# A hybrid decoder block: two more weight chunks by seven block products, and a longer split tail of the mixing layer

## The chip, the core and the metric

The kernel runs on one core of one Trainium2 chip. The metric is device time in microseconds (us) of one execution, as the median over runs. Five engines run their own instruction streams: PE (matmuls, with its weight loads shown apart as PEld), DVE, ACT and POOL for element-wise work, SP for issuing DMAs. They wait for one another by semaphores.

## The reference

One block of a decoder, 256 tokens, width 2048, all in float32. Cut to what matters here:

```python
h = rms_norm(x, norm_mix_pre)
z = h @ w_in                                     # 2048 x 11280: pool, q, k, v, low-rank gate, r, branch gates
y_a = pool_mixer(p) @ w_branch_a
o = rms_norm(gla_chunked(q, k, v, log_a), gla_norm) * silu(r)
y_b = o @ w_branch_b                             # 2048 x 2048
gates = sigmoid(gate_logits + b_branch_gates)
mixed = (gates[0] * y_a + gates[1] * y_b) @ w_out   # 2048 x 2048
x = x + rms_norm(mixed, norm_mix_post)
h = rms_norm(x, norm_ffn_pre)
f = (silu(h @ w_ffn_gate) * (h @ w_ffn_up)) @ w_ffn_down   # width 5632 between
x = x + rms_norm(f, norm_ffn_post)
```

Nearly all of the work is matrix products of the 256 tokens with large weights that are read once from memory.

## The kernel before

**Precision.** An operand is kept as two parts, a rounded high part and the remainder (`wh` and `wl` of a weight, a pair ending in h and l of an activation such as `m3h`, `m3l`). A product is three matmuls: high by high, high by the weight's remainder, and the activation's remainder by the weight's high part (lines 381 to 383 and 441 to 443). So every weight tile must be copied to `wh` by ACT (L343 or L417) and subtracted to `wl` by DVE (L347 or L421) before PE can use it.

**Jobs.** `plan()` cuts each weight into chunks of 512 columns. A chunk is a job; the order of the jobs is the order of the lists there (gates, w_branch_b, w_out, then the FFN). The weight has 16 tiles of 128 rows in k. A plain job (`fast` false) has eight steps of two k tiles each; a step multiplies both halves of the tokens (t0 and t1, 128 each) with matmuls of 512 columns: 2 k tiles x 2 halves x 3 = 12 matmuls.

**Seven block products.** A job with `fast` true takes its first eight k tiles otherwise. Tokens, k and columns are each split in two, and instead of the eight block products of that 2x2x2 cut, seven products of sums of blocks are formed, named q1, q2, q4, q6, q7, r3, r5 (class `Part`). Each is 4 k tiles x 3 = 12 matmuls of 256 columns. The sums on the weights' side are one accumulating DMA (L413, POOL's queue) and three DVE additions (L402, L404, L406); those on the activations' side are formed once per activation (`combine`). The other eight k tiles stay four steps, now with matmuls of 256 columns, 24 per step. Weights of the parts arrive as two tiles per job (`blocks`, three buffers, L1058), those of a step as one tile (`raw`, three buffers, L334); each load is 0.5 MB (512 KB), eight of them per job in either form, 4 MB in all. q1, r5, q6 and q7 are the EARLY parts: they are put between the last units of the job before (`merged`), the rest into the job's own list (`units`).

**Order and buffers.** The loop at the end of the kernel walks the units in order, and before each it prepares weights up to four units ahead, since `wh` and `wl` have four buffers (`BUFS`): the conversion of a unit waits until PE has ended the unit four before it. `blocks()` loads the next job's blocks up to twelve units ahead, when one of the three buffers is free. `done` work (evictions) is issued when a half of the tokens has its last unit; `after` and `bg` spread transposes and other side work over later units. A list scheduler of the framework then places the instructions of each engine; each engine executes its list in that order.

**The end of w_out.** `out_done` squares a chunk's result (ACT, L889) and scales it by a broadcast row (DVE, L890). In the last chunk (n = 3, here out3) `tail=3` makes the last three steps run for t0 first, all three, and then for t1. When t0 is complete, `first_residual` and `residual_part` turn t0's rows into the residual `xr` (power on POOL L211, then L913), transpose them on PE (L204, `tr<-ident,xr`) and split them into `h20h`, `h20l` and so on (L243, L244), which the first FFN gate chunk multiplies. That chunk has `head=4`: its first four steps run for t0, then for t1. In the following, out0 to out3 are the chunks of w_out, b0 to b3 those of w_branch_b, w0 to w3 the last four steps of out3, s0 to s3 the first four steps of the first FFN gate chunk.

Of the kernel before, what the change touches and what calls it, by code (L numbers as in the profile page):

```python
# [26 lines left out]
CW = 512  # L27
# [35 lines left out]
def plan():  # L63

    kt = D // P
    for kind, off, order in [("p", OFF_P, (0, 1)), ("r", OFF_R, (1, 2, 3, 0)), ("q", OFF_Q, (0, 1)), ("k", OFF_K, (0, 1))]:
        for i in order:
            low = kind == "r" and i == 0
            yield (kind, i, "w_in", 0, kt, OFF_G if low else off + i * CW, CW + RANK if low else CW,
                   kind == "r" and i > 1)  # L70
    for n in range(4):
        yield "a", n, "w_branch_a", 0, kt // 2, n * CW, CW, False
    for n in range(4):
        yield "v", n, "w_in", 0, kt, OFF_V + n * CW, CW, n > 0
    for n in range(8):
        yield "gates", n, "w_in", 0, kt, OFF_GA + n * CW, CW, n != 3
    for n in range(4):
        yield "b", n, "w_branch_b", 0, kt, n * CW, CW, n in (1, 3)
    for n in range(4):
        yield "out", n, "w_out", 0, kt, n * CW, CW, n < 3  # L80
    chunks = DFF // CW
    for part in range(3):
        ms = range(part * 4, min(part * 4 + 4, chunks))
        for m in ms:
            yield "gate", m, "w_ffn_gate", 0, kt, m * CW, CW, m > 0
            yield "up", m, "w_ffn_up", 0, kt, m * CW, CW, m > 0
        for n in range(4):
            yield "down", (part, n), "w_ffn_down", part * 16, 4 * len(ms), n * CW, CW, (part, n) != (2, 3)


def packed(name, w):

    import numpy as np

    out = []
    for _, _, which, k0, kt, c0, width, fast in plan():
        if which != name:
            continue
        rows = w[0, k0 * P:(k0 + kt) * P, c0:c0 + width].reshape(kt, P, width)
        if fast:  # L100
            for b in range(2):
                blocks = rows[b * 4:b * 4 + 4].reshape(4, P, 2, HW)
                out.append(blocks.transpose(2, 1, 0, 3).ravel())
            rows = rows[4 * FAST:]
        out.append(rows.reshape(-1, GK, P, width).transpose(0, 2, 1, 3).ravel())
    return np.concatenate(out)
# [3 lines left out]
def tile_hybrid_block(ctx: ExitStack, tc: tile.TileContext, *aps):  # L110
# [35 lines left out]
    def scratch():  # L146
        return scr.tile([P, CW], F32, tag="scr", name=nm("scr"))
# [81 lines left out]
    class Act:  # L229


        def __init__(self, name, groups, tag):
            self.name = name
            self.hi = [placed(his, (4, T), f"{tag}{g}h", f"{name}{g}h") for g in range(groups)]
            self.lo = [placed(los, (4, T), f"{tag}{g}l", f"{name}{g}l") for g in range(groups)]
# [48 lines left out]
    class Job:  # L284
# [5 lines left out]
        def __init__(self, w, at, kt, width, fast, lhs, done, across=False, head=0, tail=0, begin=None):  # L290
            self.w, self.at, self.lhs, self.kt, self.width, self.done = w, at, lhs, kt, width, done
            self.across, self.groups, self.ps, self.extra, self.fast = across, kt // GK, None, None, fast
            self.begin = begin
            both = tuple(range(NT))
            self.blocks = []
            self.early = [Part(self, n) for n in EARLY] if fast else []
            w = [Step(self, g) for g in range(FAST * 4 // GK if fast else 0, self.groups)]
            m = [(w[g], (t,)) for t in both for g in range(head)]
            m += [(x, both) for x in w[head:len(w) - tail]]
            m += [(x, (t,)) for t in both for x in w[len(w) - tail:]]  # L300
            self.units = m
            if fast:
                q2, q4, r3 = [(Part(self, n), both) for n in ("q2", "q4", "r3")]
                self.units = [q2, m[0], q4, r3] + m[1:] if len(m) > 2 else [q2, q4, r3] + m
            for w, ts in self.units:
                w.uses += 1

        def merged(self, early):

            e = [(p, (0, 1)) for p in early]  # L310
            u = self.units
            if not e:
                if self.fast and u[1][0].part:
                    u = [u[0], u[3], u[1], u[2]] + u[4:]
                return u
            if self.fast and u[1][0].part:
                return [u[0], e[0], u[1], e[1], u[2], e[2], u[3], e[3]] + u[4:]
            if self.fast:
                return u[:3] + [e[0], u[3], e[1], u[4], e[2], u[5], e[3]] + u[6:]
            u, v = u[:-4], u[-4:]  # L320
            return u + [x for pair in zip(e, v) for x in pair]
# [182 lines left out]
    def all_but_last(part, tag):  # L504
        s = one.tile([P, NT], F32, tag="ss", name=nm("ss"), bufs=2)
        dve.tensor_reduce(s, part[:, :, :3], axis=mybir.AxisListType.X, op=ALU.add)
        rs[tag] = one.tile([P, NT], F32, tag=f"ms{tag}", name=f"ms{tag}")
        dve.tensor_scalar(rs[tag], s, EPS, None, op0=ALU.add)
# [295 lines left out]
    mix = {}  # L804
# [15 lines left out]
    def broadcast(v):  # L820
        b = st.tile([P, CW], F32, tag="bc", name=nm("bc"), bufs=1)
        pool.dma_start(b, v[None, :].to_broadcast([P, CW]))
        return b
# [22 lines left out]
    def yb_done(n):  # L846
        def done(j, ts):
            if not mix:
                mix["m"] = Act("m", 4, "A")
            nat = []  # L850
            for t in ts:
                y, g = chunk(ya, t, n, "Y", "ya"), chunk(gb, t, n, "X", "gb")
                dve.tensor_tensor(g, g, j.ps[t], op=ALU.mult)
                dve.tensor_tensor(y, y, g, op=ALU.add)
                nat.append(y)
            if n == FAST - 1:
                after(3, lambda: bg.extendleft(reversed(mix["m"].combine())))
            for i in (0, 1):
                after(1 + i, lambda i=i: to_operand(mix["m"], n, nat, (i,)))
        return done  # L860
# [18 lines left out]
    def out_done(n):  # L879
        def done(j, ts):  # L880
            c = slice(n * CW, (n + 1) * CW)
            if n not in bcs:
                bcs[n] = broadcast(norm_mix_post[0, c])
            for t in ts:
                if mg[t] is None:
                    mg[t] = rest.tile([P, D], F32, tag=f"Y{t}", name=f"mg{t}")
                    xr[t] = one.tile([P, D], F32, tag=f"X{t}", name=f"xr{t}")
                    sync.dma_start(xr[t], x[0, t * P:(t + 1) * P, :])
                act.activation(scratch(), j.ps[t], AF.Square, scale=D ** -0.5, accum_out=part1[:, t, n:n + 1])  # L889
                dve.tensor_tensor(mg[t][:, c], j.ps[t], bcs[n], op=ALU.mult)  # L890
                if n == 3:
                    first_residual(t)
            if n == 2:
                all_but_last(part1, "1")
        return done

    def first_residual(t):
        r = one.tile([P, 1], F32, tag=f"rstd1{t}", name=f"rstd1{t}")
        power(r, part1[:, t, 3:], rs["1"][:, t:t + 1])
        if not h2:  # L900
            h2["h"] = Act("h2", 4, "B")
        for c in range(4):
            bg.append(lambda c=c: residual_part(t, c, r))
        if t == NT - 1:
            for c in range(4):
                bg.append(lambda c=c: squares(xr, part2, (0, 1), (c,), f32(h2["h"].lo[3][:, 3, T - 1:])))
            bg.append(second_rstd)
            bg.append(lambda: bg.extendleft(reversed(h2["h"].combine())))
# [28 lines left out]
    def ffn_gate_done(m):  # L937
        def done(j, ts):
            for t in ts:
                s = scratch()  # L940
                act.activation(s, j.ps[t], AF.Silu, scale=rz(t, "f"))
                sil[m, t] = s
        return done
# [54 lines left out]
    def finish(t, last, ps):  # L998
# [15 lines left out]
        "v": lambda n: dict(lhs=lambda: hT, done=v_done(n)),  # L1014
        "gates": lambda n: dict(lhs=lambda: hT, done=gate_done(*divmod(n, 4))),
        "b": lambda n: dict(lhs=lambda: oT["o"], done=yb_done(n)),
        "out": lambda n: dict(lhs=lambda: mix["m"], done=out_done(n), tail=3 * (n == 3)),
        "gate": lambda m: dict(lhs=lambda: h2["h"], done=ffn_gate_done(m), head=4 * (m == 0)),
        "up": lambda m: dict(lhs=lambda: h2["h"], done=ffn_up_done(m)),
        "down": lambda pn: dict(lhs=lambda: fa[pn[0]], done=down_done(*pn), tail=4 * (pn == (2, 3)),  # L1020
# [4 lines left out]
    for kind, n, name, k0, kt, c0, width, fast in plan():  # L1025
        jobs.append(Job(source[name], at[name], kt, width, fast, **kinds[kind](n)))
        at[name] += kt * P * width
# [132 lines left out]
```

## Time and profile before

| | us |
|---|---|
| three runs | 1464.76, 1464.86, 1468.63 |
| median | 1464.86 |
| the profiled execution | 1465.09 |
| its span, first to last instruction | 1463.3 |
| PE busy in it | 1439.8 |
| DVE busy in it | 1237.3 |
| ACT busy in it | 912.6 |

The profiled execution is one run of its own; 1.8 us of its time lie outside of its span. The granted clock of PE in it is 0.999 of full speed. Busy time of PE is that of overlapping instructions, so that starts of successive matmuls, and not their lengths, tell its pace.

### The profile page before, as it was taken

What the parts mean: (1) busy time and instruction counts of PE and PEld (TensorE: products, weight loads), DVE (VectorE), ACT (ScalarE), POOL (GpSimd) and SP (SyncE); (2) the same over time, 40 slices, a digit from 0 to 9 for tenths busy, and PEclk for the clock granted to TensorE, in tenths of its full rate; (3) what the DMA queues carried; (4) which work ended last, traced back from release to release, by engine and by line L of the source; (5) the groups of instructions that cost most, each with busy time, mean ns of one, the idle gap of its engine ahead of it and who ended that gap; (6) DMA issues with size and microseconds to landing.
All of it is one profiled execution on the core that took longest, in us unless ns stands there. A gap on an engine that the chain in (4) does not pass through costs nothing.

```text
span 1463.3 us, 28065 instructions
## 1 busy us (share of the span) xinstructions
PE 1439.8 (98%) x11404; PEld 1380.5 (94%) x11404; DVE 1237.3 (85%) x1390; ACT 912.6 (62%) x1192; POOL 71.3 (5%) x96
## 2 busy tenths in 40 slices
PE   8999999999999999999999999999999999999997
PEld 8999999889999899989978999999999999999996
DVE  6785568898999987899778899888989899889996
ACT  6465744556675665466557666666666666666664
POOL 2000000000100000000000000000000000000000
PEclk9999999999999999999999999999999999999999
DMA  8746566736678588648854777777766777777654
GB/s 292 261 138 218 170 218 204 240 101 215 205 221 255 187 258 265 199 168 284 265 173 159 225 221 222 225 230 235 242 215 212 224 227 232 232 238 227 205 182 149
DMA packets 89489, 316.02 MB, mean 216 GB/s; under 512 B 10204, under 2 KB 10928, under 8 KB 89104
## 3 DMA queue, kind: packets, MB, share of 16 engines
q1 hardware_dynamic: 77616, 278.89, 55.3%
q0 software_dynamic: 8448, 29.64, 10.8%
q10 hardware_dynamic: 3296, 5.71, 1.1%
q8 instruction: 89, 1.46, 0.4%
q14 instruction: 40, 0.33, 0.1%
HBM read 284.84 MB, written 4.19 MB: 198 GB/s over the span
## 4 chain that ended last, share of the span: by engine, by line
PE 78%; DVE 10%; issue 4%; DMA 3%; ACT 3%; SPq 0%; ACTq 0%; POOL 0%; DVEq 0%; POOLq 0%
PE acc L381 14%; PE acc L382 14%; PE acc L383 14%; PE ac L441 5%; PE ac L442 5%; PE ac L443 5%; PE acc L443 3%; PE acc L442 3%; PE acc L441 3%; DVE wl L421 3%; DVE wl L347 3%; PE acc L367 2%; PE acc L366 2%; PE acc L365 2%; DMA raw<-in_w_in_dram 2%
## 5 line engine op out<-in xcount | busy, mean ns | idle before, releaser
L343 ACT ACTIVATE wh<-raw 128x1024 fp32r<-128x1024 f32 (+1 forms) x328 | 347.1, 1059 | 275.1 <-PE acc L383 114.0
L347 DVE TENSOR_TENSOR wl<-raw,wh 128x1024 fp32r<-128x1024 f32 (+1 forms) x328 | 401.1, 1224 | 95.1 <-ACT wh L343 92.8
L421 DVE TENSOR_TENSOR wl<-blocks,wh 128x1024 fp32r<-128x1024 f32 x336 | 408.2, 1223 | 78.2 <-ACT wh L417 76.9
L417 ACT ACTIVATE wh<-blocks 128x1024 fp32r<-128x1024 f32 x336 | 353.4, 1059 | 162.1 <-PE acc L383 67.8
L441 PE MATMUL ac<-wh,x 128*128 128x256 f32 x420 | 116.8, 278 | 0.5 <-ACT wh L417 0.5
L442 PE MATMUL ac<-wl,x 128*128 128x256 f32 x420 | 116.2, 277 | 0.0
L443 PE MATMUL ac<-wh,x 128*128 128x256 f32 x420 | 116.1, 277 | 0.0
L382 PE MATMUL acc<-wl,h22h 128*128 128x256 f32 (+1 forms) x336 | 95.3, 284 | 1.5 <-DVE wl L347 1.5
L381 PE MATMUL acc<-wh,h22h 128*128 128x256 f32 (+1 forms) x336 | 95.7, 285 | 0.0
L381 PE MATMUL acc<-wh,h23h 128*128 128x256 f32 (+1 forms) x336 | 94.6, 282 | 0.4 <-ACT wh L343 0.4
L383 PE MATMUL acc<-wh,h22l 128*128 128x256 f32 (+1 forms) x336 | 94.9, 282 | 0.0
L383 PE MATMUL acc<-wh,h23l 128*128 128x256 f32 (+1 forms) x336 | 94.6, 282 | 0.0
L382 PE MATMUL acc<-wl,h23h 128*128 128x256 f32 (+1 forms) x336 | 94.6, 282 | 0.0
L413 POOL DMA_DIRECT2D blocks<-blocks x48 | 41.5, 865 | 904.2 <-DVE wl L347 219.6
L441 PEld LDWEIGHTS ac<-wh,x 128*128 128x128 f32 x420 | 78.9, 188 | 1.1 <-ACT wh L417 0.7
L442 PEld LDWEIGHTS ac<-wl,x 128*128 128x128 f32 x420 | 78.9, 188 | 0.5
L443 PEld LDWEIGHTS ac<-wh,x 128*128 128x128 f32 x420 | 78.9, 188 | 0.0
L382 PEld LDWEIGHTS acc<-wl,h22h 128*128 128x128 f32 x336 | 63.1, 188 | 2.8 <-DVE wl L347 2.3
L381 PE MATMUL acc<-wh,h2h 128*128 128x256 f32 (+2 forms) x224 | 65.0, 291 | 0.0
L382 PE MATMUL acc<-wl,h2h 128*128 128x256 f32 (+2 forms) x224 | 64.9, 290 | 0.0
L383 PE MATMUL acc<-wh,h2l 128*128 128x256 f32 (+2 forms) x224 | 64.9, 290 | 0.0
L383 PE MATMUL acc<-wh,h3l 128*128 128x256 f32 (+2 forms) x224 | 64.7, 289 | 0.0
(549 smaller groups left out, 4642.8 us busy)
## 6 DMA issues: line engine op xcount, KB each, us to landing
raw<-in_w_in_dram SPq DMA_DIRECT2D x120, 512.0 KB, 4.2
blocks<-in_w_in_dram SPq DMA_DIRECT2D x48, 512.0 KB, 4.5
blocks<-blocks POOLq DMA_DIRECT2D x48, 512.0 KB, 5.6
raw<-in_w_ffn_gate_dram SPq DMA_DIRECT2D x48, 512.0 KB, 4.3
raw<-in_w_ffn_up_dram SPq DMA_DIRECT2D x48, 512.0 KB, 4.3
blocks<-in_w_ffn_down_dram SPq DMA_DIRECT2D x44, 512.0 KB, 4.3
raw<-in_w_ffn_down_dram SPq DMA_DIRECT2D x44, 512.0 KB, 4.5
blocks<-in_w_ffn_gate_dram SPq DMA_DIRECT2D x40, 512.0 KB, 4.5
```

The lines of the kernel that those rows point to most:

```text
L343: act.activation(self.hi, self.raw, AF.Copy)
L347: dve.tensor_tensor(self.lo, self.raw, f32(self.hi), op=ALU.subtract)
L365: pe.matmul(dst, wh, ah, start=first and c % 2 == 0, stop=False)
L381: pe.matmul(ps, ah, hi[:, i, cs], start=first and begins, stop=False, skip_group_check=loose)
L382: pe.matmul(ps, ah, lo[:, i, cs], start=False, stop=False, skip_group_check=loose)
L383: pe.matmul(ps, al, hi[:, i, cs], start=False, stop=last and ends, skip_group_check=loose)
L413: pool.dma_start(self.block((0, 1)), self.block((0, 0)), accum_op=ALU.add)
L417: act.activation(self.hi, self.src, AF.Copy)
L421: dve.tensor_tensor(self.lo, self.src, f32(self.hi), op=ALU.subtract)
L441: pe.matmul(dst, ah, wh, start=i == 0 and p in ("q1", "r5"), stop=False, skip_group_check=True)
L442: pe.matmul(dst, ah, wl, start=False, stop=False, skip_group_check=True)
L443: pe.matmul(dst, al, wh, start=False, stop=i == 3 and p in EARLY, skip_group_check=True)
```

## The change

In `plan()` the first chunk of w_branch_b and the last chunk of w_out become `fast`. The last chunk of w_out gets `tail=4`: all its four steps behind the parts run first for t0 and then for t1, and its own parts come as q2, r3, q4 ahead of them. The second line of the `Job` class keeps `merged` from reordering such a list. The weights are packed accordingly by `packed`, on the host before the launch.

```diff
--- before.py
+++ after.py
@@ -75,9 +75,9 @@
     for n in range(8):
         yield "gates", n, "w_in", 0, kt, OFF_GA + n * CW, CW, n != 3
     for n in range(4):
-        yield "b", n, "w_branch_b", 0, kt, n * CW, CW, n in (1, 3)
+        yield "b", n, "w_branch_b", 0, kt, n * CW, CW, n in (0, 1, 3)
     for n in range(4):
-        yield "out", n, "w_out", 0, kt, n * CW, CW, n < 3
+        yield "out", n, "w_out", 0, kt, n * CW, CW, True
     chunks = DFF // CW
     for part in range(3):
         ms = range(part * 4, min(part * 4 + 4, chunks))
@@ -301,7 +301,7 @@
             self.units = m
             if fast:
                 q2, q4, r3 = [(Part(self, n), both) for n in ("q2", "q4", "r3")]
-                self.units = [q2, m[0], q4, r3] + m[1:] if len(m) > 2 else [q2, q4, r3] + m
+                self.units = [q2, r3, q4] + m if tail else [q2, m[0], q4, r3] + m[1:] if len(m) > 2 else [q2, q4, r3] + m
             for w, ts in self.units:
                 w.uses += 1
 
@@ -310,7 +310,7 @@
             e = [(p, (0, 1)) for p in early]
             u = self.units
             if not e:
-                if self.fast and u[1][0].part:
+                if self.fast and u[1][0].part and len(u) < 6:
                     u = [u[0], u[3], u[1], u[2]] + u[4:]
                 return u
             if self.fast and u[1][0].part:
@@ -1014,7 +1014,7 @@
         "v": lambda n: dict(lhs=lambda: hT, done=v_done(n)),
         "gates": lambda n: dict(lhs=lambda: hT, done=gate_done(*divmod(n, 4))),
         "b": lambda n: dict(lhs=lambda: oT["o"], done=yb_done(n)),
-        "out": lambda n: dict(lhs=lambda: mix["m"], done=out_done(n), tail=3 * (n == 3)),
+        "out": lambda n: dict(lhs=lambda: mix["m"], done=out_done(n), tail=4 * (n == 3)),
         "gate": lambda m: dict(lhs=lambda: h2["h"], done=ffn_gate_done(m), head=4 * (m == 0)),
         "up": lambda m: dict(lhs=lambda: h2["h"], done=ffn_up_done(m)),
         "down": lambda pn: dict(lhs=lambda: fa[pn[0]], done=down_done(*pn), tail=4 * (pn == (2, 3)),
```

Two places in the engines' lists. First the loads that SP issues around out3, before. `raw ... in_w_out_dram` are steps of w_out: the first is out2's third step, `raw_8139` its fourth and last, `raw_8157` the first of out3's eight; `blocks` are the parts of later FFN chunks.

```order
L334 DMA raw_8121<-in_w_out_dram 128x1024
L1058 DMA blocks_8466<-in_w_ffn_gate_dram 128x1024
L334 DMA raw_8139<-in_w_out_dram 128x1024
L1058 DMA blocks_8466<-in_w_ffn_gate_dram 128x1024
L1058 DMA blocks_8698<-in_w_ffn_up_dram 128x1024
L334 DMA raw_8157<-in_w_out_dram 128x1024
L1058 DMA blocks_8698<-in_w_ffn_up_dram 128x1024
L334 DMA raw_8187<-in_w_out_dram 128x1024
L334 DMA raw_8217<-in_w_out_dram 128x1024
L334 DMA raw_8259<-in_w_out_dram 128x1024
L334 DMA raw_8279<-in_w_out_dram 128x1024
L334 DMA raw_8297<-in_w_out_dram 128x1024
```

And in the changed kernel: `raw_8447`, `raw_8465`, `raw_8483` and `raw_8501` are w0 to w3, `raw_8601` is s0.

```order
L334 DMA raw_8447<-in_w_out_dram 128x1024
L334 DMA raw_8465<-in_w_out_dram 128x1024
L334 DMA raw_8483<-in_w_out_dram 128x1024
L1058 DMA blocks_8683<-in_w_ffn_gate_dram 128x1024 x2
L1058 DMA blocks_8916<-in_w_ffn_up_dram 128x1024 x2
L334 DMA raw_8501<-in_w_out_dram 128x1024
L334 DMA raw_8601<-in_w_ffn_gate_dram 128x1024
L334 DMA raw_8633<-in_w_ffn_gate_dram 128x1024
L334 DMA raw_8652<-in_w_ffn_gate_dram 128x1024
L334 DMA raw_8677<-in_w_ffn_gate_dram 128x1024
L334 DMA raw_8785<-in_w_ffn_gate_dram 128x1024
L334 DMA raw_8803<-in_w_ffn_gate_dram 128x1024
```

The loads of two FFN chunks' blocks, which stood between loads of early steps of out3, now stand as two pairs directly ahead of w3's load.

Second, DVE from the scaling of out3's t0 rows on, before (`mg`, line 890). `wl` are weight remainders: `wl_8358`, which stands ahead of the first scaling, is s0's, the later ones are s1 to s3.

```order
L347 TENSOR_TENSOR wl_8358<-raw_8354,wh_8356 128x1024
L890 TENSOR_TENSOR mg_7808<-acc_8265,bc_8378 128x512
L210 TENSOR_SCALAR ms_8384<-part_134,ms_8257 128x1
L913 SCALAR_TENSOR_TENSOR xr_7809<-mg_7808,rstd_8383,xr_7809 128x512 x2
L347 TENSOR_TENSOR wl_8419<-raw_8415,wh_8417 128x1024
L244 SCALAR_TENSOR_TENSOR h20l<-tr_8402,cols,h20h 128x128
L244 SCALAR_TENSOR_TENSOR h21l<-tr_8428,cols,h21h 128x128
L347 TENSOR_TENSOR wl_8445<-raw_8441,wh_8443 128x1024
L244 SCALAR_TENSOR_TENSOR h20l<-tr_8402,cols,h20h 128x128
L890 TENSOR_TENSOR mg_7814<-acc_8266,bc_8378 128x512
L244 SCALAR_TENSOR_TENSOR h21l<-tr_8428,cols,h21h 128x128
L244 SCALAR_TENSOR_TENSOR h20l<-tr_8402,cols,h20h 128x128
```

And in the changed kernel, where `wl_8605` is s0's:

```order
L890 TENSOR_TENSOR mg_7916<-acc_8259,bc_8558 128x512
L210 TENSOR_SCALAR ms_8564<-part_134,ms_8445 128x1
L913 SCALAR_TENSOR_TENSOR xr_7917<-mg_7916,rstd_8563,xr_7917 128x512 x2
L347 TENSOR_TENSOR wl_8605<-raw_8601,wh_8603 128x1024
L244 SCALAR_TENSOR_TENSOR h20l<-tr_8588,cols,h20h 128x128
L244 SCALAR_TENSOR_TENSOR h21l<-tr_8620,cols,h21h 128x128
L347 TENSOR_TENSOR wl_8637<-raw_8633,wh_8635 128x1024
L244 SCALAR_TENSOR_TENSOR h20l<-tr_8588,cols,h20h 128x128
L244 SCALAR_TENSOR_TENSOR h21l<-tr_8620,cols,h21h 128x128
L913 SCALAR_TENSOR_TENSOR xr_7917<-mg_7916,rstd_8563,xr_7917 128x512
L244 SCALAR_TENSOR_TENSOR h20l<-tr_8588,cols,h20h 128x128
L244 SCALAR_TENSOR_TENSOR h21l<-tr_8620,cols,h21h 128x128
```

The remainder of s0 has moved from ahead of t0's scaling to behind t0's first residuals, and the scaling of t1's rows (before, the second `L890`) is not yet among these twelve rows.

## Rows read from the trace of the kernel before

**Rows 1.** The page's first part: span, then busy time of each engine.
```profile
span 1463.3 us, 28065 instructions
...
PE 1439.8 (98%) x11404; PEld 1380.5 (94%) x11404; DVE 1237.3 (85%) x1390; ACT 912.6 (62%) x1192; POOL 71.3 (5%) x96
```

**Rows 2.** Windows: stretch, length, busy of PE, PEld, DVE, ACT, POOL; clock; DMA.
```profile
647.00:676.00 29.00, 28.05 (x237) 27.54 (x236) 28.62 (x33) 17.71 (x22) 0.87 (x1) 1.00 0.75 241
...
719.00:750.00 31.00, 30.69 (x175) 26.27 (x174) 16.88 (x20) 14.39 (x20) 1.97 (x3) 1.00 0.77 251
750.00:775.00 25.00, 23.87 (x111) 17.42 (x110) 21.65 (x48) 17.12 (x40) 1.72 (x2) 1.00 0.51 159
```

**Rows 3.** Timeline of PE: start, length, instruction; four first matmuls of units.
```profile
575.10 0.39 PE L381 MATMUL acc<-wh,o0h 128*128 128x512 f32 x1
...
586.08 0.28 PE L441 MATMUL ac<-wh,o0h 128*128 128x256 f32 x1
...
692.24 0.28 PE L441 MATMUL acc<-wh,m1h 128*128 128x256 f32 x1
...
712.64 0.28 PE L441 MATMUL acc<-wh,m1h 128*128 128x256 f32 x1
```

**Rows 4.** Timeline of PE around the transposes of b0's and b2's results.
```profile
604.44 0.28 PE L383 MATMUL acc<-wh,o2l 128*128 128x256 f32 x1
604.77 0.30 PE L204 MATMUL tr<-ident,ya 128*128 128x128 f32 x1
...
651.88 0.30 PE L204 MATMUL tr<-ident,ya 128*128 128x128 f32 x1 [0.84 <-DVE ya L854]
```

**Rows 5.** Timeline of ACT at the end of out1 (712) and of out3's t0.
```profile
712.16 0.60 ACT L889 ACTIVATE scr<-acc 128x512 f32<-128x512 f32 x1 [0.43 <-PE acc L383]
...
713.42 1.05 ACT L417 ACTIVATE wh<-blocks 128x1024 fp32r<-128x1024 f32 x1
...
745.65 0.60 ACT L889 ACTIVATE scr<-acc 128x512 f32<-128x512 f32 x1 [3.06 <-PE acc L383]
```

**Rows 6.** Timeline of DVE at the same two places, and behind the second.
```profile
711.75 1.23 DVE L421 TENSOR_TENSOR wl<-blocks,wh 128x1024 fp32r<-128x1024 f32 x1 [0.34 <-ACT wh L417]
712.90 1.35 DVE L890 TENSOR_TENSOR mg<-acc,bc 128x512 f32<-128x512 f32 x2
...
730.54 0.15 DVE L506 TENSOR_REDUCE ss<-part 128x2 f32<-128x6 f32 x1
730.72 0.17 DVE L508 TENSOR_SCALAR ms<-ss 128x2 f32<-128x2 f32 x1
...
746.37 0.69 DVE L890 TENSOR_TENSOR mg<-acc,bc 128x512 f32<-128x512 f32 x1 [2.52 <-ACT scr L889]
...
747.86 1.41 DVE L913 SCALAR_TENSOR_TENSOR xr<-mg,rstd,xr 128x512 f32<-128x512 f32 x2 [0.68 <-POOL rstd L211]
...
756.81 2.07 DVE L913 SCALAR_TENSOR_TENSOR xr<-mg,rstd,xr 128x512 f32<-128x512 f32 x3
```

**Rows 7.** Loads of w_out, all, least, median and most us to landing.
```profile
DMA to landing us min/median/max: 3.2/5.2/7.7
```

**Rows 8.** SP's timeline, a pair; then the issue of 690.70, us to landing.
```profile
689.52 0.80 SPq L1058 DMA_DIRECT2D blocks<-in_w_out_dram  x2
...
raw<-in_w_out_dram SPq DMA_DIRECT2D x1, 512.0 KB, 7.2
```

**Rows 9.** DMA issues of 717.2 to 719.4, the second load of a pair.
```profile
blocks<-in_w_ffn_up_dram SPq DMA_DIRECT2D x1, 512.0 KB, 6.1
```

**Rows 10.** Timeline of PE from out3's last t0 matmul to the gate chunk's t1.
```profile
745.45 0.39 PE L381 MATMUL acc<-wh,m2h 128*128 128x512 f32 x1
...
748.67 0.33 PE L204 MATMUL tr<-ident,xr 128*128 128x128 f32 x1 [0.31 <-DVE xr L913]
...
750.42 0.39 PE L381 MATMUL acc<-wh,h20h 128*128 128x512 f32 x1
...
758.88 0.50 PE L381 MATMUL acc<-wh,h20h 128*128 128x512 f32 x1
```

## The prediction

> **What bounds the kernel now.** I read the page's first part, then windows, then PE's timeline unit by unit. PE is busy for 1439.8 of 1463.3 us [rows 1], DVE is next at 85%. That is an average, so I look at the stretches that the change touches: from the third w_branch_b chunk on DVE is the fuller one for a while (28.62 of 29 us, with PE at 28.05), at the end of w_out PE has 30.69 of 31, and in the 25 us behind it PE loses over a microsecond of busy time while DVE is at 21.65 [rows 2]. So a saving of PE columns is worth its full size in w_branch_b and w_out, unless a weight is late there; and the seam from w_out to the FFN is a chain through DVE, where PE waits.
>
> PE's pace: from 575.10 to 586.08 b0 issues 48 matmuls of 512 columns, 229 ns each; from 692.24 to 712.64, a whole job by seven products, 180 matmuls of 256 columns go by, 113.3 ns each, with no gap [rows 3].
>
> **The change part by part.** All times below are against the profiled execution of 1465.09 us, span 1463.3, and 0.2 above the median of the runs.
>
> b0, columns. A plain job is 96 x 229 ns = 21.98 us. By seven products it is 180 x 113.3 ns = 20.40 us (84 matmuls in the parts, 96 in the steps). Saved: 1.58 us. Loads are 4 MB in both forms. DVE gets three more remainders and three block sums, 6 x 1.23 = 7.4 us, and two small evictions; PE's 20.4 us have room for it, as out1 shows, which does the same without a gap in 20.40 us [rows 3]. Where the results of a w_branch_b chunk are transposed, PE waits for DVE already: behind b0 0.33 us from a matmul to the transpose instead of 0.11, so 0.22, and behind b2 0.84 [rows 4]. With DVE fuller ahead of it I book 0.1 us more behind b0; the bounds are 0 and 0.8, the wait behind b2, where DVE is fullest.
>
> out3, columns. The same exchange: 1.58 us saved if every wait stays as it is. The four EARLY parts move into out2's list, where PE and DVE work as in out1.
>
> out3, the weight of w3. This is the new wait that I expect. Four half steps follow each other at 12 x 113.3 ns = 1.36 us, so PE eats weights twice as fast as in a full step, and all four must be there before t1 begins. I take time 0 where out2 ends and read the offsets from the end of out1, at 712.64, which is the same seam between two such jobs. ACT's two squares begin 0.48 us before it and its next conversion at +0.78 [rows 5]; DVE's two scalings start at +0.26 and end at +1.61 [rows 6]. Behind out2 two small reductions follow (0.15 + 0.17) [rows 6], so DVE takes w0's remainder at +1.95 and ends at +3.2. There are three raw buffers, and w3's load goes into w0's: it leaves SP at +3.2. It then needs its landing L, a conversion of 1.05 on ACT and 1.23 on DVE [rows 5, 6], about 2.4 with handovers: w3 is ready at +5.6 + L. PE has q2, r3, q4 and the t0 halves of w0 to w2 ahead of it, 6 x 1.36 = 8.16 us. So PE waits L - 2.6 us. For L the trace gives 3.2 at the least, 5.2 in the median, 7.7 at the most [rows 7], and 7.2 for a load that left at 690.70, 1.2 us behind the first of a pair of blocks [rows 8]. In the changed list two pairs stand directly ahead of w3's load. The second pair waits for q4's remainder, which ends at +0.34 (711.75 + 1.23 against 712.64) [rows 6]; the second of such a pair lands 6.1 us after its issue [rows 9], so near +6.8 (its own issue is at +0.7), and w3, issued behind it on the same queue, later still. I take L = 4.3, which is +7.5 and between the least and the median, since nothing but that pair is left in front of it: a wait of 1.7 us. Its bounds are 0.6 (L = 3.2) and 5.1 (L = 7.7).
>
> Beside this row the Trainium skill ("DMA: Bandwidth & Descriptors", Issuing engines are not separate DMA queues) says that transfers run on the same 16 DMA engines whichever engine started them, and interleave. By it the broadcast row that POOL fetches for out3 at that moment slows w3's load as well, which is a reason against the lower bound; no row here separates the two.
>
> The seam to the FFN. t0's last product ends near 745.45, PE meets the first transpose of the residual at 748.67 after a wait of 0.31, starts the gate chunk at 750.42 and its t1 half at 758.88, that is 13.43 us after t0's end [rows 10]. t1's residuals start on DVE at 756.81, 11.36 after t0's end [rows 6]; from the first scaling at 746.37 DVE's list up to there holds two scalings, four residuals, eight splits and three remainders. In the changed list it is the same with four remainders: s0's weights could be prepared ahead of t0's end with three steps in the tail, and cannot be with four, since all four buffers are held until w0's t1 half is over. So DVE's chain grows by 1.23 us. PE's own work between the two points grows by 4 x 1.36 - 3 x 6 x 0.229 = 1.32 us, t1's longer tail, which covers the chain. The two nearly cancel: t1 would start at 13.43 + 1.23 = 14.7 by the chain, and at 14.75 with PE's waits as they were. As s0's conversion must also wait for w0's t1 half, 1.36 us after t0's end, I book +0.2; the bounds are -1.3 (the longer tail covers what PE waits for, the remainder finds a hole in DVE's list) and +0.9 (DVE waits for ACT between its pieces).
>
> The sum: -1.58 + 0.1 - 1.58 + 1.7 + 0.2 = -1.16, so -1.2 us. The rest of the program, FFN included, keeps its lists. From the median of 1464.86 this is 1463.7 us.
>
> On the columns a rule speaks against the change. The Trainium skill ("TensorE: Matmul & The Clock Gate", Back-to-back issue gap) gives an isolated matmul at full clock N / 2.4 ns plus about 2.5 ns, so every one of the 84 extra matmuls would cost a fixed piece. The trace does not agree: 229 ns for 512 columns is more than twice 113.3.
>
> **The rivals.**
>
> A, both savings arrive. L is 3.2 since nothing is left in the queue, and t1's longer tail covers the seam: -3.16 + 0.1 + 0.6 - 1.3 = -3.8, 1461.1 us. For it: at the seam PE waits for what DVE makes (0.31 for the first residual [rows 10]), and more cover would hide some of that. Against it: the two pairs ahead of w3, and the fourth remainder in the chain.
>
> B, w3 comes late and the kernel is slower. If L is 7.7, PE waits 5.1, and with the seam at +0.9 the sum is -3.16 + 0.1 + 5.1 + 0.9 = +2.9, 1467.8 us. It decides from L = 5.5 on, where the sum is zero. For it: 7.2 behind one pair [rows 8], and here two pairs. Against it: that load left 1.2 us behind its pair, w3's leaves about 2.9 behind the start of the nearer one.
>
> C, DVE is the bound in w_branch_b. b0, b1's EARLY parts and b0's results then cost 0.8 more, and so does b1's end: -1.16 + 1.5 = +0.3, 1465.2 us. For it: 28.62 of 29 [rows 2]. Against it: that stretch also forms the sums of the new activation, which b0's does not.
>
> D, a fixed cost per matmul. If each of the 84 extra matmuls of a job cost 6 ns in these chunks, 0.5 us per job, the sum is -1.16 + 1.0 = -0.2, 1464.7 us. For it speaks only that 113.3 ns was read in another chunk; against it, that out1 has 180 of them in 20.40 us [rows 3]. It is the formula of the Trainium skill above, by which 256 columns take 109.2 ns, 512 take 215.8, and a job saves 1.06 us.
>
> **How the numbers follow.** The forecast has 0.50, A 0.18, B 0.20, C 0.10, D 0.02. The forecast's own range is L from 3.6 to 5.0 and the seam from -0.5 to +0.6, so -2.6 to -0.2: 1462.3 to 1464.7 us. The range of 8 in 10 reaches to A and most of B: 1460.9 to 1467.5. About 0.3%, 4.4 us, is what a measurement of this kernel can tell from no change. Only A with a little more gets past -4.4, 0.05 in all; B past +4.4 needs a second mishap, 0.05; within 0.3% remains 0.90.
>
> **What would show it.** In the changed kernel's trace: b0 in 180 matmuls of 113 ns, some 1.5 us shorter; no new gap in out2; the copy of w3 on ACT with idle time before it that a w_out load ended, and PE waiting between w2's and w3's t0 halves, 1 to 2.5 us; from t0's end to the gate chunk's t1 half 14.5 to 15.2 us instead of 13.43. I am wrong if w3's wait is under 0.6 or over 3 us, if the seam is shorter than 13.4, or if PE shows gaps in b0 or b1 of more than a microsecond.

## The result and the profile after

The changed kernel takes 1468.35 us (median of 20 runs) against 1465.28 us of the kernel before (20 runs). The ratio is 1.0016, 95% interval 1.001 to 1.0022: slower by 2.3 us, between 1.5 and 3.2. Forecast were 1463.7 us and a range up to 1467.5; the time lies above it, and the sign is wrong. The forecast started from 1464.86, the median of three runs of the kernel before; the median of twenty is 0.4 us higher. The medians of the two kernels differ by 3.1 us, the means of the same runs by 2.4, which is nearer to the ratio.

The profiled execution took 1468.22 us. The page's first part, as in [rows 1]:

```profile
span 1466.3 us, 28455 instructions
...
PE 1439.3 (98%) x11572; PEld 1387.5 (95%) x11572; DVE 1252.5 (85%) x1406; ACT 921.1 (63%) x1206; POOL 72.7 (5%) x98
```

PE has less busy time than before and the span is 3.0 us longer, so PE waits more or runs slower; the totals do not say where.

PE's timeline (start, length, instruction, and in brackets the idle time before it and who ended it) shows b0's q2, its first step, and the start of b1's q2, where b0's list ends.

```profile
581.64 0.28 PE L441 MATMUL acc<-wh,o1h 128*128 128x256 f32 x1
583.00 0.28 PE L381 MATMUL acc<-wh,o2h 128*128 128x256 f32 x1
...
602.04 0.28 PE L441 MATMUL acc<-wh,o1h 128*128 128x256 f32 x1
```

602.04 - 581.64 = 20.40 us: 180 matmuls at 113.3 ns with no gap. That was the price booked, instead of the 21.98 us that a plain job takes at the pace of [rows 3].

PE's timeline at out3 shows q2, the last t0 product of w2, the first two of w3, four of the following ones, t1's second matmul (the first, 743.59, went into the wait), and the gate chunk's t1 half.

```profile
732.41 0.28 PE L441 MATMUL acc<-wh,m1h 128*128 128x256 f32 x1
...
740.46 0.28 PE L383 MATMUL acc<-wh,m3l 128*128 128x256 f32 x1
743.36 0.39 PE L381 MATMUL acc<-wh,m3h 128*128 128x256 f32 x1 [2.63 <-ACT wh L343]
743.59 0.28 PE L381 MATMUL acc<-wh,m2h 128*128 128x256 f32 x1
744.62 0.38 PE L382 MATMUL acc<-wl,m3h 128*128 128x256 f32 x1 [0.76 <-DVE wl L347]
...
744.96 0.42 PE L381 MATMUL acc<-wh,m3h 128*128 128x256 f32 x1
745.17 0.42 PE L382 MATMUL acc<-wl,m3h 128*128 128x256 f32 x1
...
746.67 0.41 PE L383 MATMUL acc<-wh,m3l 128*128 128x256 f32 x1
746.89 0.41 PE L382 MATMUL acc<-wl,m2h 128*128 128x256 f32 x1
...
761.21 0.50 PE L381 MATMUL acc<-wh,h20h 128*128 128x512 f32 x1 [0.46 <-ACT h20h L243]
```

The expected wait is there, in two pieces: from start to start 2.90 and 1.03 us, less a matmul each, so 2.79 for w3's high part and 0.92 for its remainder, 3.7 in all instead of 1.7. Then something that was not expected: 744.96 to 745.17 is 0.21 us from one matmul of 256 columns to the next, nearly twice 113 ns. The windows say why (stretch, length, busy of PE, PEld, DVE, ACT, POOL; granted clock; DMA share; GB/s):

```profile
740.00:743.30 3.30, 0.73 (x7) 0.53 (x5) 0.00 (x0) 1.04 (x1) 0.00 (x0) 1.00 1.05 375
744.90:748.20 3.30, 3.30 (x18) 3.30 (x18) 0.36 (x1) 0.69 (x2) 0.00 (x0) 0.51 0.54 170
```

Behind the wait PE has 0.51 of its clock, the 1.2 GHz level, for 3.3 us. In the wait DVE is idle and the DMA engines are full. What ACT waited for was w3's load (its row among the DMA issues follows, with the us to landing):

```profile
742.25 1.06 ACT L343 ACTIVATE wh<-raw 128x1024 fp32r<-128x1024 f32 x1 [5.86 <-DMA raw<-in_w_out_dram]
```

```profile
raw<-in_w_out_dram SPq DMA_DIRECT2D x1, 512.0 KB, 6.3
```

So L was 6.3 us, not 4.3. The load left SP at 735.53. The engines were not full all that time:

```profile
737.00:738.50 1.50, 1.50 (x15) 1.50 (x15) 0.78 (x1) 0.00 (x0) 0.00 (x0) 1.00 0.39 117
738.50:741.80 3.30, 2.23 (x20) 2.03 (x18) 0.00 (x0) 0.00 (x0) 0.85 (x1) 1.00 0.98 381
```

From 737.0 to 738.5, when the second pair had landed, they moved 117 GB/s, and 381 GB/s from there to w3's landing.

### The profile page after: what moved, and what is told of

Read it like the earlier page. It is cut to its first block, busy times and chain, and to the rows that moved or that the text cites. A ratio compares the mean times of both kernels' runs of the same rounds, so it can differ in the third digit from the quotient of the medians.

```text
span 1466.3 us, 28455 instructions
## 1 busy us (share of the span) xinstructions
PE 1439.3 (98%) x11572; PEld 1387.5 (95%) x11572; DVE 1252.5 (85%) x1406; ACT 921.1 (63%) x1206; POOL 72.7 (5%) x98
## 4 chain that ended last, share of the span: by engine, by line
PE 82%; DVE 9%; ACT 3%; DMA 3%; issue 3%; SPq 0%; ACTq 0%; DVEq 0%
PE acc L381 15%; PE acc L382 15%; PE acc L383 14%; PE ac L441 6%; PE ac L442 6%; PE ac L443 5%; PE acc L443 4%; PE acc L441 4%; PE acc L442 4%; DVE wl L421 3%; DVE wl L347 2%; PE acc L367 2%; PE acc L366 2%; PE acc L365 2%; DMA raw<-in_w_in_dram 2%
## 5 line engine op out<-in xcount | busy, mean ns | idle before, releaser
L343 ACT ACTIVATE wh<-raw 128x1024 fp32r<-128x1024 f32 (+1 forms) x320 | 338.6, 1059 | 259.2 <-PE acc L383 112.2
L421 DVE TENSOR_TENSOR wl<-blocks,wh 128x1024 fp32r<-128x1024 f32 x350 | 425.0, 1222 | 80.8 <-ACT wh L417 79.3
L417 ACT ACTIVATE wh<-blocks 128x1024 fp32r<-128x1024 f32 x350 | 368.1, 1059 | 168.7 <-PE acc L383 70.9
L347 DVE TENSOR_TENSOR wl<-raw,wh 128x1024 fp32r<-128x1024 f32 (+1 forms) x320 | 390.8, 1223 | 81.8 <-ACT wh L343 79.5
L441 PE MATMUL ac<-wh,x 128*128 128x256 f32 x432 | 120.1, 278 | 0.5 <-ACT wh L417 0.5
L442 PE MATMUL ac<-wl,x 128*128 128x256 f32 x432 | 119.6, 277 | 0.0
L443 PE MATMUL ac<-wh,x 128*128 128x256 f32 x432 | 119.5, 277 | 0.0
L413 POOL DMA_DIRECT2D blocks<-blocks x50 | 43.2, 864 | 899.8 <-DVE wl L347 187.1
L441 PEld LDWEIGHTS ac<-wh,x 128*128 128x128 f32 x432 | 81.1, 188 | 1.1 <-ACT wh L417 0.7
L443 PEld LDWEIGHTS ac<-wh,x 128*128 128x128 f32 x432 | 81.2, 188 | 0.0
```

The costliest lines, as they stand in the source:

```text
L343: act.activation(self.hi, self.raw, AF.Copy)
L347: dve.tensor_tensor(self.lo, self.raw, f32(self.hi), op=ALU.subtract)
L413: pool.dma_start(self.block((0, 1)), self.block((0, 0)), accum_op=ALU.add)
L417: act.activation(self.hi, self.src, AF.Copy)
L421: dve.tensor_tensor(self.lo, self.src, f32(self.hi), op=ALU.subtract)
L441: pe.matmul(dst, ah, wh, start=i == 0 and p in ("q1", "r5"), stop=False, skip_group_check=True)
```

## The experiments

All times are against the kernel before, timed beside each kernel. Theory 1 is that w3's late landing and what follows from it are the whole loss, and that the columns bring what was booked.

**b0 alone.** The last chunk of w_out as before.

```diff
-    yield "out", n, "w_out", 0, kt, n * CW, CW, True
+    yield "out", n, "w_out", 0, kt, n * CW, CW, n < 3
-    ... done=out_done(n), tail=4 * (n == 3)),
+    ... done=out_done(n), tail=3 * (n == 3)),
```

> Only the first w_branch_b chunk goes by seven products; w_out and its tail of three steps are as before. Theory 1 (the loss of the changed kernel sits at w3's late weight and what follows it; the columns bring what was booked): b0 takes 20.40 us instead of 21.98 and the transposes behind it cost 0.1 to 0.2 more, so -1.5 us against the kernel before, about 1463.8. Theory 2 (the changed kernel loses in w_branch_b too, since DVE or the loads ahead of b0 give the columns back): 0 to +1 us against the kernel before.

Measured: ratio 0.9991 (0.9981 to 1.0001), -1.3 us. The middle is theory 1's; a loss of a microsecond is excluded, but that b0 gains nothing is not.

**out3 alone.** b0 plain.

```diff
-    yield "b", n, "w_branch_b", 0, kt, n * CW, CW, n in (0, 1, 3)
+    yield "b", n, "w_branch_b", 0, kt, n * CW, CW, n in (1, 3)
```

> Only the last w_out chunk goes by seven products, with its tail of four; b0 is a plain chunk as before. Theory 1: this half carries the whole loss: PE waits 3.7 us for w3's weight and has half its clock for some 3 us behind the wait, so the sum is the changed kernel's +2.3 us and the 1.5 us that b0 saved, +3.8 us against the kernel before. Theory 2 (b0 is a loser of +1): +1.3 us.

Measured: ratio 1.0029 (1.0017 to 1.004), +4.2 us. The loss is in this half. PE's timeline shows the same two waits, and the windows the lower clock, which set in at the end of the first wait:

```profile
747.46 0.58 PE L381 MATMUL acc<-wh,m3h 128*128 128x256 f32 x1 [2.89 <-ACT wh L343]
...
748.72 0.58 PE L382 MATMUL acc<-wl,m3h 128*128 128x256 f32 x1 [0.46 <-DVE wl L347]
```

```profile
748.00:750.00 2.00, 1.54 (x8) 1.28 (x7) 0.67 (x1) 0.00 (x0) 0.00 (x0) 0.50 0.84 168
750.00:752.00 2.00, 2.00 (x11) 2.00 (x11) 0.00 (x0) 0.53 (x2) 0.00 (x0) 0.50 0.70 227
```

**w3 in a buffer of its own.** Its load leaves 2.9 us before the first pair.

```diff
+    if j.w is w_out and j.tail and self.g == 7:
+        self.raw = two_st.tile([P, 2, 4, P], F32R, tag="K0", ...)   # viewed as 128 x 2 x 512
+    else:
         self.raw = wp.tile([P, GK, j.width], F32, tag="raw", ..., bufs=RAWS)
```

> Both chunks as in the changed kernel, but w3's weight is loaded into memory of its own (a buffer of the o activation's combinations, dead by then), so its load leaves long before the block pairs. Theory 1 (w3's landing is the cause, and the clock falls because PE stands still): no wait between w2's and w3's t0 halves, no stretch at half clock, 3.7 us of waits and 1.0 us of slow matmuls ahead of t0's end are gone; the seam stays 14 to 14.6 us, set by DVE. That is the changed kernel -4.7, or -2.4 us against the kernel before. Rival (the clock falls for another reason, such as the many matmuls before): the 3.7 us go, but a stretch at half clock stays near t0's end, -1.4 us against the kernel before. Rival (DVE's chain to the FFN takes back what PE gains): about 0 against the kernel before.

Measured: ratio 0.9987 (0.9978 to 0.9995), -1.9 us: faster than both kernels. PE from out3's q2 to the last t0 product, t1's first one and the gate chunk's t1 half (lines are three higher here):

```profile
735.70 0.28 PE L444 MATMUL acc<-wh,m1h 128*128 128x256 f32 x1
...
745.10 0.28 PE L386 MATMUL acc<-wh,m3l 128*128 128x256 f32 x1
745.22 0.28 PE L384 MATMUL acc<-wh,m2h 128*128 128x256 f32 x1
...
759.54 0.50 PE L384 MATMUL acc<-wh,h20h 128*128 128x512 f32 x1 [0.46 <-ACT h20h L243]
```

745.22 - 735.70 = 9.52 us, which is 84 matmuls at 113.3 ns: no wait, no slow stretch. In the changed kernel the same stretch takes 746.89 - 732.41 = 14.48. The seam is 14.32 us in both, so PE's pace does not set it, and the slow matmuls behind t0's end cost nothing there. That DVE's chain sets it instead is the prediction's account; no run isolates it. Theory 1 expected -2.4, the two rivals -1.4 and 0; the interval excludes the third, and the trace shows no stretch at the lower clock, on which the second rested.

**The pairs behind w3.** A tiny copy makes the two pairs wait for w3's landing.

```diff
+    if counts_["low"] in (317, 324):
+        pool.tensor_copy(tile_[:, :, 0, :1], order[312].raw[:, :, :1])
     for i in range(2):
         sync.dma_start(tile_[:, i], ...)
```

> The changed kernel, but the two pairs of FFN blocks wait for w3's landing (a copy of two values per partition from w3's weight into the blocks' buffer), so that they are issued behind w3's load; w3 still waits for w0's buffer. Theory 1a (w3 lands late because of the 2 MB ahead of it on the queue): L falls from 6.3 us to between 3.2 and 4.3, PE waits 0.6 to 1.7, and the sum is about 2.5 us below the changed kernel or more, 0 to -2 us against the kernel before. Rival (L is long because of the loads issued beside and behind it, s0's, s1's and POOL's broadcast row): L stays at 5.5 or more, PE waits 3 us or more, and the time is that of the changed kernel within 1 us.

Measured: ratio 0.9992 (0.9983 to 1.0001), -1.2 us. The load, PE, and two windows:

```profile
raw<-in_w_out_dram SPq DMA_DIRECT2D x1, 512.0 KB, 4.9
```

```profile
741.23 0.39 PE L381 MATMUL acc<-wh,m3h 128*128 128x256 f32 x1 [1.17 <-ACT wh L343]
...
742.49 0.39 PE L382 MATMUL acc<-wl,m3h 128*128 128x256 f32 x1 [0.88 <-DVE wl L347]
```

```profile
736.70:739.80 3.10, 3.10 (x30) 3.10 (x28) 0.40 (x1) 0.00 (x0) 0.00 (x0) 1.00 0.91 341
742.00:744.00 2.00, 1.51 (x12) 1.51 (x13) 0.43 (x1) 0.00 (x0) 0.00 (x0) 1.00 0.71 211
```

L fell, though not to the 4.3 that theory 1a allowed at most, nor did it stay at the rival's 5.5, and the clock stayed up. In four traces with the pairs ahead L is 6.3, 6.9, 6.6 and 6.8: they cost 1.4 to 2.0 us. The rest has another cause. The windows show what the pairs do: w3's load left at 734.86 here, and the engines move 341 GB/s from 1.8 us behind it on; with the pairs ahead that takes 3.0 us, and the 1.5 us before have a DMA share of 0.39. By this the pairs make w3's data start later, more than they share the engines with it; why, was not tried. POOL's accumulating load (L413), which a pair's landing sets off, goes with the pairs too, but it is no rival: in the changed kernel it was issued at 739.15, and all of POOL's queue moved 0.05 of the 1.26 MB between 738.5 and 741.8.

**s0 and s1 behind w3 too.** Their loads wait as well, by the same tiny copy into their `raw`.

> As the kernel with the block pairs behind w3's landing (there L was 4.9 us and PE waited 2.5), and the loads of s0 and s1, which it issued 1.1 and 2.3 us behind w3's, wait for w3's landing too. Theory (loads issued behind w3 share the 16 engines with it): L falls to 3.2 to 4.2 and PE's wait to 0.6 to 1.6 us. Rival (only what stands ahead, or POOL's broadcast row beside it, delays w3): L stays between 4.6 and 5.2. s0's and s1's weights come 4 us later, so the time may rise by what the gate chunk then waits; the trace tells.

**And the row away.** POOL's row for out3 gets memory of its own and is fetched early.

> As the kernel before in this list (pairs, s0 and s1 behind w3's landing), and POOL's broadcast row for out3 is fetched early into memory of its own, so that w3's load is alone. If the row shares too, L is 3.2 us, the least of the rows of the kernel before, and 0.5 or more below the kernel without this step; if the row does not matter, L is as there within 0.3 us.

Measured, one trace each for L: 4.4 and 4.1 us, the first between what theory (up to 4.2) and rival (from 4.6) allowed.

```profile
raw<-in_w_out_dram SPq DMA_DIRECT2D x1, 512.0 KB, 4.4
```

```profile
raw<-in_w_out_dram SPq DMA_DIRECT2D x1, 512.0 KB, 4.1
```

Times: 0.9993 (0.9981 to 1.0004) and 1.0003 (0.999 to 1.0016). Loads issued behind w3's add about 0.5 us to its landing, the row 0.3 or nothing; a POOL row of the FFN, fetched at 732.91 in the last of these, may still have shared, so 3.2 was not reached. The steps of 0.5 and 0.3 rest on a single trace each.

In the first of the two the clock fell, behind the shorter waits:

```profile
741.48 0.39 PE L383 MATMUL acc<-wh,m3h 128*128 128x256 f32 x1 [0.67 <-ACT wh L345]
742.73 0.38 PE L384 MATMUL acc<-wl,m3h 128*128 128x256 f32 x1 [0.87 <-DVE wl L349]
```

```profile
743.30:746.60 3.30, 3.30 (x18) 3.30 (x17) 0.79 (x2) 0.69 (x2) 0.00 (x0) 0.50 1.05 361
```

So the shorter L brought nothing: q2 to t0's end takes 12.37 us, with 12.15 in the kernel that has only the pairs behind.

**The wait filled.** 26 matmuls without use between w2's and w3's t0 halves.

```diff
+    if w.j.w is w_out and w is w.j.units[-1][0] and ts == (0,):
+        idle, ah, banks["at"] = bank(), w.j.lhs().get(12, 0)[0], banks["at"] - 1
+        for _ in range(26):
+            pe.matmul(idle[:, :HW], ah, units[n - 1][1].hi[:, 0, :HW], start=True, stop=True)
     w.multiply(ts)
```

> The changed kernel, with 26 matmuls of 256 columns whose results nobody reads put on PE between w2's and w3's t0 halves (26 x 113 ns = 2.9 us, the length of the wait for w3's first weight part). Theory (the clock fell because PE stood still): the granted clock stays at 1.00 behind the wait, the matmuls from w3's second on go by at 113 ns instead of 214, t0 ends 1.0 us earlier, and the time is 0.5 to 1 us below the changed kernel, +1.3 to +1.8 against the kernel before. Rival (the clock falls for what came before or for another reason): a stretch at half clock stays, and the time is that of the changed kernel or above it, +2.3 to +3.

Measured: ratio 1.0014 (1.0005 to 1.0022), +2.1 us: too close to the changed kernel's 2.3 to tell by time. The trace tells:

```profile
738.50 3.11 PE L1104 MATMUL tr<-wh,m3h 128*128 128x256 f32 x26
...
742.86 0.39 PE L382 MATMUL acc<-wl,m3h 128*128 128x256 f32 x1 [0.87 <-DVE wl L347]
```

```profile
743.00:746.00 3.00, 3.00 (x26) 3.00 (x27) 0.81 (x2) 0.81 (x3) 0.00 (x0) 1.00 0.73 203
```

With PE kept at work the clock stays at 1.00, 26 matmuls go by in the 3 us behind, and q2 to t0's end takes 744.26 - 730.34 = 13.92 us instead of 14.48, with L at 6.6. This goes with the theory, that the clock fell because PE stood still, but it is one trace, and the clock stays up behind some waits that nobody filled, as the next run shows.

**A tail of three.** `tail=3`, the rest as in the change.

> The changed kernel with tail=3: out3's parts, then w0 for both halves, then w1 to w3 for t0, then for t1. PE has one half step (1.36 us) more ahead of w3, and s0's weight may be made ahead of t0's end as in the kernel before. Theory (w3's landing decides): PE waits 3.7 - 1.36 = 2.3 us, the clock stays up as it did with 2.5 us of waits, the seam is 13.4 us again, so -1.5 - 1.58 + 2.3 = -0.8 us against the kernel before. Rival (the four-step tail is what costs, by the held buffers and the fourth remainder in DVE's chain): the seam falls by more than a microsecond beyond its shorter tail and the time is -2 us or less. Rival (the clock falls with any wait for w3): +0.2 us.

Measured: ratio 1.0013 (1.0001 to 1.0024), +1.9 us. The trace goes with the theory, but L was 6.8 here:

```profile
743.85 0.39 PE L381 MATMUL acc<-wh,m3h 128*128 128x256 f32 x1 [1.75 <-ACT wh L343]
...
745.11 0.39 PE L382 MATMUL acc<-wl,m3h 128*128 128x256 f32 x1 [0.87 <-DVE wl L347]
```

```profile
745.00:748.00 3.00, 2.89 (x24) 2.89 (x25) 1.76 (x3) 0.69 (x2) 0.00 (x0) 1.00 0.77 209
```

There are two waits, the clock is at 1.00, and the seam is 13.4. The time is 2.7 us above the -0.8 expected; the longer L explains 0.5, the rest stays open.

**A plain chunk with a tail of four.** b0 fast, out3 as before but `tail=4`.

> b0 by seven products, out3 a plain chunk as in the kernel before, but with tail=4. Half steps take 2.75 us, so every weight is there in time. It measures what the tail of four costs by itself. Theory (the tail costs nothing or less; the loss came from w3's weight): no wait ahead of t0's end, and the seam from t0's end to the gate chunk's t1 half grows by no more than the 2.75 us of PE's work that moved behind t0, so -1.5 to -2.3 us against the kernel before. Rival (the fourth remainder in DVE's chain costs at the seam): -0.6 us or above, with the seam longer than 16.2 us.

Measured: ratio 0.9993 (0.9985 to 1.0002), -1.0 us, between the two. By the trace t0 ends 0.8 us earlier (17.07 us after out3's start instead of 17.85; w3's remainder is 0.5 late) and the seam is 14.91 instead of 13.43. So the tail of four costs a plain chunk 0.7 us; how much of it comes from w3's late remainder and how much from DVE's chain was not separated.

**Own buffer and a tail of three.**

> As the kernel with a buffer of its own for w3's weight (both chunks by seven products), but with tail=3. Theory (without w3's wait the tail's length hardly matters: t0 ends 1.36 us later and the seam is shorter by the half step of t1 and by what the fourth remainder costs): within 0.5 us of the same kernel with tail=4, -1.9 to -3 us against the kernel before. Rival (the tail of four costs DVE's chain a remainder of 1.23 us): 1 us or more below the kernel with tail=4.

Measured: ratio 0.9981 (0.9973 to 0.999), -2.8 us. q2 to t0's end is 10.88 us, the seam 13.43. This is the best of the kernels run, though its interval overlaps that of the tail of four, and by the traces its stretch from q2 to the gate chunk is 0.5 us longer (24.31 against 23.84). Which of the two is better stays open.

**Own buffer and b2 by seven products**, with a tail of four, then of three (`n in (0, 1, 3)` becomes `True`).

> A version meant to beat both: w3's weight in a buffer of its own, tail of four, and the last plain chunk of w_branch_b (b2) by seven products too. If DVE has room, 1.58 us less than without b2: -3.5 us against the kernel before. If DVE is the bound from b1 to b3 (the rival of the prediction on w_branch_b), the gain is half of it or less, or a loss: -1 to -2.5.

> The same with a tail of three. By the traces t0 ends 1.36 us later and the seam is 0.9 us shorter, so 0.5 us above the tail of four; by the runs of the kernels without b2 it was 0.9 below. Either way within 1 us of the tail of four.

Measured: 1.0004 (0.9995 to 1.0013) and 1.0008 (0.9998 to 1.0017): no gain, where -1 to -3.5 us were expected; the two lie within 1 us of each other, as expected. By the traces the stretch from b0's first matmul to the first of w_out takes 91.6 and 91.0 us, against 88.2 in the own-buffer kernels with b2 plain. With b2 fast, DVE is full where the new activation's sums are formed, and PE stands and then runs at the lower clock (tail of four):

```profile
648.37 0.38 PE L385 MATMUL acc<-wl,o2h 128*128 128x256 f32 x1 [1.79 <-DVE wl L350]
```

```profile
646.00:648.00 2.00, 0.57 (x5) 0.37 (x4) 2.00 (x3) 1.44 (x3) 0.00 (x0) 1.00 0.27 49
...
650.00:652.00 2.00, 2.00 (x11) 2.00 (x11) 2.00 (x4) 0.00 (x0) 0.00 (x0) 0.50 0.95 371
```

With a tail of three PE stands at the same place for as long, and the clock stays up:

```profile
649.39 0.38 PE L385 MATMUL acc<-wl,o2h 128*128 128x256 f32 x1 [1.84 <-DVE wl L350]
```

```profile
650.00:652.00 2.00, 2.00 (x20) 2.00 (x20) 2.00 (x4) 0.65 (x1) 0.00 (x0) 1.00 1.02 395
```

## Why the prediction was wrong

The stretch from out3's q2 to the gate chunk's t1 half sums it up. The seam is the time from t0's end to that t1 half, and the sum is the two together. The kernel before takes 31.29 us from out3's start; less the 1.58 saved and the 5.44 of the four parts that move into out2, 24.27 would be the columns alone.

| kernel | q2 to t0's end | seam | sum | L | clock behind the wait |
|---|---|---|---|---|---|
| columns alone | | 13.43 | 24.27 | | |
| the changed kernel | 14.48 | 14.32 | 28.80 | 6.3 | 0.51 |
| out3 alone | 14.98 | 14.76 | 29.74 | 6.9 | 0.50 |
| the wait filled | 13.92 | 14.32 | 28.24 | 6.6 | 1.00 |
| tail of three | 14.09 | 13.41 | 27.50 | 6.8 | 1.00 |
| pairs behind w3 | 12.15 | 14.70 | 26.85 | 4.9 | 1.00 |
| s0 and s1 behind w3 too | 12.37 | 14.40 | 26.77 | 4.4 | 0.50 |
| and the row away | 11.35 | 14.32 | 25.67 | 4.1 | 1.00 |
| own buffer | 9.52 | 14.32 | 23.84 | | no wait |
| own buffer, tail of three | 10.88 | 13.43 | 24.31 | | no wait |

- **b0, columns: right.** 20.40 us, no gap. From b0's start to out0's, with the moved EARLY parts set right, the trace has 1.73 us less than before; forecast was 1.48, and with b0 alone it is 1.45. The transposes behind b0 cost 0.14 more and those behind b1 0.3, but the wait of 0.84 behind b2 [rows 4] went away. That last is luck: the wait is 0.45 with b0 alone and 0.04 with out3 alone. Rival C did not come here; with b2 fast as well it did.
- **out3, columns: right.** The own buffer's 9.52 us have nothing in them but matmuls at 113.3 ns.
- **The wait for w3: right in form, wrong in size. This is the step that failed.** "PE waits L - 2.6": with L = 6.3 that is 3.7, and 3.7 was measured; with 4.9 it is 2.3, measured 2.5. But "I take L = 4.3 [...] since nothing but that pair is left in front of it" was wrong. The second pair landed 6.1 us after out2's end, sooner than assumed, and w3 still came 3.3 us behind it, not 0.7: w3's data had hardly begun to move when the pair had landed (117 GB/s in all from 737.0 to 738.5), and then s0's and s1's loads, issued 1.1 and 2.3 us behind w3's, and POOL's row shared the engines with it (share 0.98, and 0.5 us less with s0 and s1 away). Rows at hand pointed there: 7.2 behind one pair [rows 8]. The mis-sizing is 2.0 us. The Trainium skill ("DMA: Bandwidth & Descriptors", Issuing engines are not separate DMA queues) says that DMAs started by the scalar, sync or gpsimd engine run on the same 16 DMA engines and interleave; that L falls from 4.4 to 4.1 with POOL's row away goes with it, on one trace. The prediction used this against its lower bound alone. The larger steps, 6.3 to 4.9 and 4.9 to 4.4, are of loads on SP's own queue. The prediction's own sign of being wrong, a wait of more than 3 us, came.
- **The clock: not in the sum.** The wait was priced as idle time. Behind 2.63 and 0.76 us of standing PE ran at 0.51, and the 11 matmuls from 744.62 to t0's end took 2.27 us instead of 1.25: +1.0. That the standing caused it is argued and not shown by one run: in the traces at hand the clock falls in the middle of the kernel five times, each time directly at waits of PE of 1.5 us or more, in one piece or two, and never at out3 where nothing waited or the wait was filled. But not every such wait brings it down. The Trainium skill ("TensorE: Matmul & The Clock Gate", Part 1: The HAM clock gate) says that an idle array gets half its clock and activity gives it back; the trace agrees with 0.51, and with 1.00 when the wait is filled; the 1.00 behind 1.75 + 0.87 us of standing is not told by it.
- **The seam: nearly right.** 14.32 us, between the 13.43 of before and the 14.7 of the chain. Against PE's longer tail (+1.32) that is -0.43, where +0.2 was booked and -1.3 to +0.9 allowed.

Out3's side is then -1.58 + 4.96 - 0.43 = +3.0 (4.96 is 14.48 - 9.52: the 3.7, the 1.0 and what lies between), b0's side -1.7: +1.2 by the trace, +1.5 to +3.2 by the runs. In the two profiles 1.1 us more lie ahead of b0 (581.64 against 575.10 + 5.44) and some 0.7 behind 770, in lists that did not change; b0's q2 starts at 579.24, 580.88, 581.64 and 584.93 in four traces with the same lists ahead of it, so it cannot be put down to the change. Whether the missing microsecond is a longer L in most runs stays open. It is no more than one trace can miss: reckoned alike for the other kernels of the table (the sum less the 31.29 - 5.44 of the kernel before, and less b0's 1.45 where b0 is fast), the measured differences lie from 0.7 below to 2.1 above what the traces give; for the own buffer -1.9 was measured and the trace gives -3.5. What happened is rival B, which decides from L = 5.5 on; it got 0.20. The range ended at 1467.5, because B was priced without the clock and reached only in part. (The forecast's own range ends at -3.16 + 0.1 + 2.4 + 0.6 = -0.1, not at -0.2; nothing hangs on it.)

## What to carry to other kernels

When faster arithmetic eats weights faster, follow the last weight's load back to the buffer it waits for and to every load issued around it, ahead and behind; its landing is that of the busy queue, not the median. A wait of the matmul engine costs its length and can cost a stretch at the lower clock behind it; matmuls without use in the wait kept the clock up in the one trace that tried it. A dead buffer of the right size can be worth more than the saved columns: here it turned +2.3 us into -1.9.

## What the runs showed of the hardware

The clock fell behind waits of 2.63 + 0.76 and 0.67 + 0.87 us, at the end of the first of 2.89 + 0.46, and, in w_branch_b, behind 1.79 us; it stayed at 1.00 behind 1.17 + 0.88 and 1.75 + 0.87, and behind 1.84 us at the same place in w_branch_b. The fifth fall, with the tail of three, stands at 481 us behind a wait of 1.93 us. So the idle time alone does not tell it; what does was not tried. The slow stretches lasted 3.3 us and more, though PE was busy again. A load of 512 KB needed 6.3 to 6.9 us to land behind two pairs of such loads, 4.9 without them, 4.4 with the two loads behind it away too, and 4.1 without the row; behind the pairs, the engines moved 117 GB/s in the 1.5 us until the second had landed, 3.0 us after the load's issue, and 381 from there on.
